# Three score regions side by side in five PSUM banks, and a group's products with v in one batch

## The chip, the cores and the metric

The kernel runs on one core of a Trainium2 chip. The metric is the device time of one execution in microseconds (us); lower is better. The kernel before took 2687.36 us, the median of three runs (2685.77 to 2690.11). The engines named here are TensorE (PE, with its weight loads as PEld), VectorE (DVE), ScalarE (ACT), GpSimd (POOL) and SyncE (SP), which issues loads. [...]

## The reference

A two-layer diffusion block (512 latent tokens, 256 context tokens, width 1024) and then a third layer of recurrent mixers. Only the two attentions matter here. The first layer has 16 query heads of 64 in 4 groups that share keys and values; the second has 16 heads of 96 with keys and values of their own. Both attend without a mask.

```python
def block_attention(q, k, v):            # q (B, Sq, KVH, G, dk); k (B, T, KVH, dk); v (B, T, KVH, dv)
    scale = dk ** -0.5
    qb = jnp.moveaxis(q.reshape(b, nb, Q_BLOCK, kvh, g, dk), 1, 0)     # blocks of 128 queries
    def one_block(qi):
        s = jnp.einsum('bqhgd,bkhd->bhgqk', qi, k, preferred_element_type=jnp.float32) * scale
        p = jax.nn.softmax(s, axis=-1).astype(v.dtype)
        return jnp.einsum('bhgqk,bkhe->bqhge', p, v)
    o = lax.map(one_block, qb)
    return jnp.moveaxis(o, 0, 1).reshape(b, sq, kvh * g * v.shape[-1])

# layer 0: y_lat = block_attention(q_lat, k_all, v_all) @ w_o, y_ctx = block_attention(q_ctx, k_ctx, v_ctx) @ w_o
# layer 1: y_lat alone; k_all holds 512 latent and 256 context keys
```

## The kernel before

Both attentions are run by one function, `attend`, over a list of units. A unit is one block of 128 queries of one head against its 768 keys; four units are a group (`GqaGroup`: four heads that share keys, in the first attention; `MlaHead`: four query blocks of one head, in the second). The first attention has 64 such units and then 16 context units, each two heads against the 256 context keys, of which two are a group. The second has 64 units.

The order is written by hand (`manual_schedule`), as a software pipeline over n. In step n stand, one behind the other:

- the casts out of PSUM that are left from step n-1 (`highs`, on ScalarE, some on VectorE);
- the exponential of unit n-1 (`exps`, ScalarE, L631), which also sums its row;
- the transposes of unit n-4's probabilities (`turn`, TensorE L660, or L653 for context), copied out by ScalarE (four blocks) and VectorE (two) in L661 and L655;
- the scores of unit n (TensorE, L716 or L1013), their row maximum (VectorE, L603) and the scaled negative maximum (L680 or L997);
- the reciprocal of unit n-1's row sum (VectorE, L637) and the scaling of its probabilities (POOL, L640);
- the subtractions left from step n-1 (`late`, VectorE);
- the stage work of step n: the queries of a later group are transposed (L698, cast in L702 and L703, subtracted in L706 and L707); in the second attention K and V (`kproj`, `vproj`), Q (`qproj`) and its turned rope part (`qrot`) of later heads are computed, with copies out of PSUM on ScalarE (L1271, L1284, L1296, L1309) and, for K and Q of the next head, three casts (L1319) and three subtractions (L1323) on VectorE;
- a part of a finished group's products with v (`products`, TensorE L722 or L1021, on half-width tiles of 64 columns), `per` keys in a step: two of six in the first attention, one of two for context, three of six in the second. When the last is done, the cast of the result (ScalarE, L734 or L1034) and the subtraction for its low part (VectorE, L738 or L1040) follow in the next step.

PSUM is laid out by pools: two score tiles `s` of two banks each, used in turn, and four tiles of one bank under the tag `pt`, for transposes, projections and the group's products `ob`. The framework puts in the waits: an instruction waits for those that touch the same tile before it. A wait is left out where an earlier one on the same engine covers it.

Each fp32 product with v is two instructions in the trace, so that a group of six blocks of keys and two halves has 24. Matrix products elsewhere are three instructions each (L139 to L141), of high and low parts.

Of the kernel before, what the change touches and what calls it, by code (L numbers as in the profile page):

```python
# [9 lines left out]
F32 = mybir.dt.float32  # L10
# [6 lines left out]
PSUM = bass.MemoryType.PSUM  # L17
P = 128
# [8 lines left out]
class Bump:  # L27


    def __init__(self, *regions):  # L30
        self.free = list(regions)
        self.tags = {}
# [273 lines left out]
class GqaNet(Base):  # L306
# [103 lines left out]
    def gqa(self):  # L410
        nc, i, tc, flow = self.nc, self.i, self.tc, self.flow
        W = i["gqa_w_qkv"][0]
        with ExitStack() as ph:
# [6 lines left out]
            with tc.tile_pool(name="q0", bufs=1, reuse_waits="tile") as pool, tc.tile_pool(name="q0ps", bufs=2, reuse_waits="tile", space=PSUM) as ps:  # L420
# [46 lines left out]
                b = self.turn_cols(rows, ps, pool, "b")  # L467
# [52 lines left out]
                            flow.add(ada.pop(0))  # L520
                flow.finish()
                self.ada_bufs = 2
            with tc.tile_pool(name="a0", bufs=1, reuse_waits="tile") as pool, tc.tile_pool(name="a0s", bufs=2, reuse_waits="tile", space=PSUM) as pss, \
                    tc.tile_pool(name="a0p", bufs=4, reuse_waits="tile", space=PSUM) as psp:
                units = []
                for ts in (range(4), (4, 5)):
                    for o in range(2):
                        for t in ts:
                            for g in (2 * o, 2 * o + 1):
                                gr = GqaGroup(self, pool, Q, K, V, t, g)  # L530
                                units += [(gr, (x,)) for x in range(4)] if t < 4 else [(gr, (0, 1)), (gr, (2, 3))]
                stages = {}
                none = lambda: None
                for n, (gr, xs) in enumerate(units):
                    if xs[0] == 0:
                        stages.setdefault(n - 3, []).append(gr.prepare(psp))
                n = 8
                for t in range(6):
                    for f in self.q_rope(None, Q, t, 1):
                        stages.setdefault(n, []).append((f, none, none))  # L540
                        n += 2
                ada = self.ada_steps(0, 11, pool, psp, None, True)
                next(ada)
                for x in range(2):
                    stages.setdefault(1 + x, []).insert(0, (lambda: next(ada, None), none, none))
                self.ahead = []
                for x in range(2):
                    for y, f in enumerate(self.out_weights(i["gqa_w_o"][0], x)):
                        stages.setdefault(n - 2 + 6 * x + 2 * y, []).append((f, none, none))
                self.attend(units, pool, pss, psp, stages)  # L550
# [18 lines left out]
    def attend(self, units, pool, pss, psp, stages):  # L569

        nc = self.nc
        N = len(units)
        work, highs, lows = [], [], []
        for n in sorted(k for k in stages if k < 0):
            for fs in stages[n]:
                for f in fs:
                    f()
        with self.tc.manual_schedule():  # L580
            for n in range(N + LAG + 6):
                for f in highs:
                    f()
                highs, late, lows = [], lows, []
                if 1 <= n <= N:
                    self.exps(pool, *units[n - 1])
                if LAG < n <= N + LAG and units[n - LAG - 1][0].last == units[n - LAG - 1][1][-1]:
                    g, xs = units[n - LAG - 1]
                    g.ob = psp.tile([P, 2, 128], F32, name="ob", tag="pt")
                    work.append((g, g.products()))  # L590
                if LAG <= n < N + LAG:
                    g, xs = units[n - LAG]
                    self.turn(pool, psp, g, xs)
                if n < N:
                    g, xs = units[n]
                    s = pss.tile([P, 1024], F32, name="s", tag="s")
                    m = self.sp.tile([P, 3, 2], F32, name="sm", tag="sm", bufs=6)
                    for k, x in enumerate(xs):
                        g.scores(x, s[:, k * g.nk:(k + 1) * g.nk])
                    if n == 0:  # L600

                        nc.scalar.activation(self.sp.tile([P, 1], F32, name="se", tag="se", bufs=1), s[:, :1], AF.Exp, scale=0.0)
                    nc.vector.tensor_reduce(out=m[:, 0, :len(xs)], in_=s[:, :g.nk * len(xs)]  # L603
                                            .rearrange("p (k n) -> p k n", k=len(xs)), axis=AX.X, op=ALU.max)
                    g.sm[xs] = s, m
                    g.bias(xs, m)
                if 1 <= n <= N:
                    self.softmax_end(*units[n - 1])
                for f in late:
                    f()  # L610
                for pe, high, low in stages.get(n, []):
                    pe()
                    highs.append(high)
                    lows.append(low)
                if work:
                    g, fs = work[0]
                    for f in fs[:g.per]:
                        f()
                    del fs[:g.per]
                    if not fs:  # L620
                        work.pop(0)
                        highs.append(g.high)
                        lows.append(g.low)
            assert not work and not highs and not lows

    def exps(self, pool, g, xs):
# [37 lines left out]
class GqaGroup:  # L664


    def __init__(self, net, pool, Q, K, V, t, g):
        self.net, self.pool, self.Q, self.K, self.V, self.t, self.g = net, pool, Q[t], K, V, t, g
        self.c0, self.nk = (0, NL + NC) if t < 4 else (NL, NC)
        self.keys = list(range(6)) if t < 4 else [4, 5]  # L670
        self.p, self.sm, self.last = {}, {}, 3
        self.per = 2 if t < 4 else 1

    def scale(self, x):
        return self.net.RS[:, self.t, 4 * self.g + x:4 * self.g + x + 1]
# [32 lines left out]

        return turn, high, low

    def scores(self, x, s):
        q = self.q[x % 2][:, 128 * (x // 2):128 * (x // 2) + 128]
        for j in range(2):
            for n0 in range(0, self.nk, 512):
                n1 = min(self.nk, n0 + 512)
                self.net.nc.tensor.matmul(s[:, n0:n1], lhsT=q, rhs=self.K[j][:, self.g, self.c0 + n0:self.c0 + n1],  # L716
                                          start=j == 0, stop=j == 1)

# [265 lines left out]
class MlaHead:  # L984

    last = 3
    per = 3

    def __init__(self, m, h):
        self.m, self.net, self.h, self.nk = m, m.net, h, NL + NC  # L990
# [13 lines left out]
            self.pT.append(pool.tile([P, 6, 2, 128], F32, name="pT", tag="pT", bufs=3))  # L1004
        return self.pT[x // 2][:, :, x % 2, :]

    def scores(self, x, s):
        e = self.h % 2
        (qh, ql), (kh, kl) = self.m.Q[e], self.m.K[e]
        c = slice(128 * x, 128 * x + 128)  # L1010
        for k, (a, b) in enumerate(((qh, kh), (qh, kl), (ql, kh))):
            for n0, n1 in ((0, 512), (512, 768)):
                self.net.nc.tensor.matmul(s[:, n0:n1], lhsT=a[:, c], rhs=b[:, n0:n1], start=k == 0, stop=k == 2)  # L1013

    def products(self):
# [32 lines left out]
class MlaNet(MlpNet):  # L1048
    def mla(self):
        nc, i, tc = self.nc, self.i, self.tc  # L1050
        m = Mla(self)
        self.m = m
        with ExitStack() as ph:
            mp = ph.enter_context(tc.tile_pool(name="mp", bufs=1, reuse_waits="tile"))
            tcf = [T.rearrange("p a b -> p (a b)") for T in self.TC]
            xf = self.XN.rearrange("p a b -> p (a b)")
            m.cqT = [mp.tile([P, 3, NL], F32R, name=f"cqT{j}") for j in range(2)]
            m.ckT = [t[:, :1536].rearrange("p (k n) -> p k n", k=2) for t in tcf]
            m.qpe = xf[:, :2048].rearrange("p (t h f) -> p t h f", t=4, h=16)


            kk = mp.tile([P, 2, 2, NL + NC], F32R, name="K")
            m.K = [[kk[:, e, j, :] for j in range(2)] for e in range(2)]
            m.Q = [[tcf[j][:, 1536:] for j in range(2)], [mp.tile([P, NL], F32R, name=f"Q1{j}") for j in range(2)]]
            with tc.tile_pool(name="mA", bufs=1, reuse_waits="tile") as pool:
                self.mla_in(pool, m, kk.rearrange("p e j n -> p (e j n)"))
            self.l0.close()
            with tc.tile_pool(name="a1", bufs=1, reuse_waits="tile") as pool, tc.tile_pool(name="a1s", bufs=2, reuse_waits="tile", space=PSUM) as pss, \
                    tc.tile_pool(name="a1p", bufs=4, reuse_waits="tile", space=PSUM) as psp:
                self.mla_attend(pool, pss, psp, m.cqT, m.ckT, m.qpe, m)  # L1070

    def row_rs(self, pool, x, n):
# [1625 lines left out]
```

## Time and profile before

| | us |
|---|---|
| median of three runs | 2687.36 |
| profiled execution | 2689.55 |
| its span, first to last instruction | 2687.7 |
| TensorE busy in it | 2588.1 (96%) |
| VectorE busy | 1734.3 (65%) |
| ScalarE busy | 1156.9 (43%) |
| POOL busy | 649.7 (24%) |

The profiled execution is 2.2 us above the median, and its time lies 1.9 us above its span. The first attention lies at about 159 to 349 us of the span, the second at about 1064 to 1304. A busy TensorE in the profile is not one at its peak: ends of matmuls are modelled, and matmuls overlap. Of several waits of one instruction the profile names the one that came last.

### The profile page before, as it was taken

How to read it: one execution, taken by the hardware profiler on the slowest of the kernel's cores; microseconds unless marked ns; L12 is line 12 of the kernel's file. 1: busy time of each engine (PE TensorE's matmuls, PEld its weight loads, DVE VectorE, ACT ScalarE, POOL GpSimd, SP SyncE). 2: the span in 40 equal slices, each digit the busy share in tenths (PEclk: the TensorE clock that was granted, in tenths of full speed). 3: DMA queues.
4: the chain of work that ended last, by engine and by line, in shares of the span. 5: the costliest groups of instructions: out<-in, count | busy, mean ns of one | idle time of the engine just before them, and what ended most of it. 6: DMA issues, size and time to landing. Idle time of an engine off the chain costs nothing. (4 is left out here: it accounts for less than half of the span.)

```text
span 2687.7 us, 37906 instructions
## 1 busy us (share of the span) xinstructions
PE 2588.1 (96%) x14954; PEld 2118.7 (79%) x14954; DVE 1734.3 (65%) x3102; ACT 1156.9 (43%) x2016; POOL 649.7 (24%) x541
## 2 busy tenths in 40 slices
PE   8999999999999999999999899989999999999998
PEld 5666689888888898777787678877678888888887
DVE  4458847876666577788488987576675533534445
ACT  4357835333333235655364344253563223532222
POOL 0224322233322013333134445043140011000000
PEclk9999999999999999999999999999999999999999
DMA  8510221333333112000255454234123234222221
GB/s 317 205 32 1 66 92 34 124 120 126 118 122 101 62 39 69 19 33 17 64 166 172 138 174 158 95 107 117 46 68 102 86 94 137 75 94 94 94 94 63
DMA packets 178644, 264.83 MB, mean 99 GB/s; under 512 B 18019, under 2 KB 116954, under 8 KB 177954
## 3 DMA queue, kind: packets, MB, share of 16 engines
q1 hardware_dynamic: 173010, 257.89, 29.0%
q10 hardware_dynamic: 5456, 4.51, 0.6%
q8 instruction: 118, 1.93, 0.3%
q14 instruction: 60, 0.49, 0.1%
HBM read 256.81 MB, written 5.58 MB: 98 GB/s over the span
## 5 line engine op out<-in xcount | busy, mean ns | idle before, releaser
L129 DVE TENSOR_TENSOR wl<-raw,wh 128x1024 fp32r<-128x1024 f32 (+1 forms) x301 | 397.7, 1334 | 358.8 <-ACT wh L126 355.9
L126 ACT CAST wh<-raw 128x1024 fp32r<-128x1024 f32 (+1 forms) x301 | 306.7, 1034 | 618.8 <-PE mm L140 449.7
L139 PE MATMUL mm<-TL,wh 128*128 128x512 f32 (+2 forms) x1512 | 565.7, 375 | 6.1 <-ACT TL L387 4.7
L140 PE MATMUL mm<-TL,wh 128*128 128x512 f32 (+2 forms) x1512 | 561.5, 372 | 4.5 <-DVE TL L388 4.4
L141 PE MATMUL mm<-TL,wl 128*128 128x512 f32 (+2 forms) x1512 | 560.1, 371 | 0.0
L139 PEld LDWEIGHTS mm<-TL,wh 128*128 128x128 f32 (+1 forms) x1512 | 287.2, 190 | 60.5 <-ACT TL L387 5.6
L140 PEld LDWEIGHTS mm<-TL,wh 128*128 128x128 f32 (+1 forms) x1512 | 287.7, 190 | 54.8 <-DVE TL L388 6.0
L141 PEld LDWEIGHTS mm<-TL,wl 128*128 128x128 f32 (+1 forms) x1512 | 287.3, 190 | 52.5
L139 PE MATMUL mm<-TC,wh 128*128 128x256 f32 (+1 forms) x672 | 223.6, 333 | 7.8 <-ACT low L867 7.8
L640 POOL TENSOR_SCALAR p<-p,sm 128x768 f32<-128x768 f32 (+1 forms) x160 | 156.1, 978 | 297.0 <-DVE sm L637 201.9
L141 PE MATMUL mm<-TC,wl 128*128 128x256 f32 (+1 forms) x672 | 223.0, 332 | 0.0
L140 PE MATMUL mm<-TC,wh 128*128 128x256 f32 (+1 forms) x672 | 222.8, 332 | 0.0
L258 POOL TENSOR_TENSOR XN<-XN 128x512 f32<-128x512 f32 x84 | 132.4, 1594 | 282.4 <-ACT XN L251 279.6
L139 PE MATMUL mm<-gh,wh 128*128 128x256 f32 (+1 forms) x544 | 179.7, 330 | 0.3 <-DVE RL L878 0.3
L140 PE MATMUL mm<-gl,wh 128*128 128x256 f32 (+1 forms) x544 | 178.7, 329 | 0.0
L141 PE MATMUL mm<-gh,wl 128*128 128x256 f32 (+1 forms) x544 | 178.1, 328 | 0.0
L258 POOL TENSOR_TENSOR low<-low 128x512 f32<-128x512 f32 x84 | 136.0, 1632 | 152.9 <-ACT low L251 150.1
L603 DVE TENSOR_REDUCE sm<-s 128x1 f32<-128x768 f32 (+1 forms) x144 | 132.7, 922 | 22.5 <-PE s L1013 11.4
L139 PEld LDWEIGHTS mm<-TC,wh 128*128 128x128 f32 x672 | 127.5, 190 | 23.3 <-ACT low L867 9.1
L140 PEld LDWEIGHTS mm<-TC,wh 128*128 128x128 f32 x672 | 127.6, 190 | 13.9
L141 PEld LDWEIGHTS mm<-TC,wl 128*128 128x128 f32 x672 | 127.6, 190 | 12.7
L660 PE MATMUL pt<-ident,p 128*128 128x128 f32 x768 | 116.0, 281 | 17.5 <-ACT pT L661 7.8
(614 smaller groups left out, 4978.8 us busy)
## 6 DMA issues: line engine op xcount, KB each, us to landing
raw<-in_mlp_w_dram SPq DMA_DIRECT2D x64, 1024.0 KB
raw<-in_w_in_dram SPq DMA_DIRECT2D x26, 1024.0 KB
XN<-in_w_ada_dram SPq DMA_DIRECT2D x24, 1024.0 KB
low<-in_ada_w_dram SPq DMA_DIRECT2D x24, 1024.0 KB
raw<-in_ffn_w_in_dram SPq DMA_DIRECT2D x22, 1024.0 KB
adaw<-in_w_ada_dram SPq DMA_DIRECT2D x21, 1024.0 KB
raw<-in_ffn_w_out_dram SPq DMA_DIRECT2D x11, 1024.0 KB
raw<-in_gqa_w_qkv_dram SPq DMA_DIRECT2D x6, 1024.0 KB
```

The costliest lines, as they stand in the source:

```text
L126: nc.scalar.copy(h, v)
L129: nc.vector.tensor_tensor(l, v, h, op=ALU.subtract)
L139: nc.tensor.matmul(out, lhsT=ah, rhs=bh, start=start, stop=False)
L140: nc.tensor.matmul(out, lhsT=ah, rhs=bl, start=False, stop=False)
L141: nc.tensor.matmul(out, lhsT=al, rhs=bh, start=False, stop=stop)
L258: nc.gpsimd.tensor_tensor(rows[k], rows[k], rows[k + h], op=ALU.add)
L603: nc.vector.tensor_reduce(out=m[:, 0, :len(xs)], in_=s[:, :g.nk * len(xs)] .rearrange("p (k n) -> p k n", k=len(xs)), axis=AX.X, op=ALU.max)
L640: nc.gpsimd.tensor_scalar(out=g.p[xs][:, c], in0=g.p[xs][:, c], scalar1=m[:, 2, k:k + 1], scalar2=1.0, op0=ALU.mult, op1=ALU.mult)
L660: nc.tensor.transpose(tp[:, 128 * (x - lo):128 * (x - lo) + 128], p[:, 128 * x:128 * x + 128], self.ident)
```

## The change

There is one PSUM tile S of 2560 columns (five banks) for the whole of an attention. Unit n's scores go to columns 768 (n mod 3) and on: region 0 has bank 0 and the first half of bank 1, region 1 the second half of bank 1 and bank 2, region 2 bank 3 and the first half of bank 4. The products of a group go to the last 256 columns, the second half of bank 4. [...] The products of a group are issued in one step. Tiles under the tag `pt` are three instead of four.

```diff
-            with ... tc.tile_pool(name="a0s", bufs=2, reuse_waits="tile", space=PSUM) as pss, \
-                    tc.tile_pool(name="a0p", bufs=4, reuse_waits="tile", space=PSUM) as psp:
+            with ... tc.tile_pool(name="a0s", bufs=1, reuse_waits="tile", space=PSUM) as pss, \
+                    tc.tile_pool(name="a0p", bufs=3, reuse_waits="tile", space=PSUM) as psp:
...
         work, highs, lows = [], [], []
+
+        S = pss.tile([P, 2560], F32, name="s", tag="s")
...
-                    g.ob = psp.tile([P, 2, 128], F32, name="ob", tag="pt")
+                    g.ob = S[:, 2304:].rearrange("p (a n) -> p a n", a=2)
                     work.append((g, g.products()))
...
-                    s = pss.tile([P, 1024], F32, name="s", tag="s")
+                    c0 = 768 * (n % 3)
+                    s = S[:, c0:c0 + 768]
                     m = self.sp.tile([P, 3, 2], F32, name="sm", tag="sm", bufs=6)
                     for k, x in enumerate(xs):
-                        g.scores(x, s[:, k * g.nk:(k + 1) * g.nk])
+
+                        a, b = c0 + k * g.nk, c0 + (k + 1) * g.nk
+                        cut = min(b, (a // 512 + 1) * 512)
+                        g.scores(x, s[:, k * g.nk:(k + 1) * g.nk], [(p - a, q - a) for p, q in ((a, cut), (cut, b)) if q > p])
...
                 if work:
-                    g, fs = work[0]
-                    for f in fs[:g.per]:
+
+                    g, fs = work.pop(0)
+                    for f in fs:
                         f()
-                    del fs[:g.per]
-                    if not fs:
-                        work.pop(0)
-                        highs.append(g.high)
-                        lows.append(g.low)
+                    highs.append(g.high)
+                    lows.append(g.low)
...
-    def scores(self, x, s):
+    def scores(self, x, s, cuts):
         q = self.q[x % 2][:, 128 * (x // 2):128 * (x // 2) + 128]
         for j in range(2):
-            for n0 in range(0, self.nk, 512):
-                n1 = min(self.nk, n0 + 512)
+            for n0, n1 in cuts:
                 self.net.nc.tensor.matmul(s[:, n0:n1], lhsT=q, rhs=self.K[j][:, self.g, self.c0 + n0:self.c0 + n1],
                                           start=j == 0, stop=j == 1)
```

The same two pool lines change for the second attention, and its `scores`. Line numbers behind the edit move by one to four: the score lines L716 and L1013 become L718 and L1014, the maximum L603 becomes L609, the exponential L631 becomes L635, the products L722 and L1021 become L724 and L1022, their casts L734 and L1034 become L736 and L1035, their subtractions L738 and L1040 become L740 and L1041.

TensorE in the first attention, in the middle of a group, before (`s` scores, `ob` products, `pt` transposes; in brackets the engines whose signals an instruction waits for):

```order
L722 MATMUL ob<-pT,V 64x256 x4
L660 MATMUL pt<-ident,p 128x128 [waits DVE_49,Pool_49]
L660 MATMUL pt<-ident,p 128x128 x3
L660 MATMUL pt<-ident,p 128x128 [waits Activation_49]
L660 MATMUL pt<-ident,p 128x128
L716 MATMUL s<-K_86,q_2105 128x512
L716 MATMUL s<-K_86,q_2105 128x256
L716 MATMUL s<-K_87,q_2105 128x512
L716 MATMUL s<-K_87,q_2105 128x256
L722 MATMUL ob<-pT,V 64x256 x4
L660 MATMUL pt<-ident,p 128x128 [waits DVE_49,Pool_49]
```

And now, in a unit with products:

```order
L718 MATMUL s<-K_86,q_2076 128x512 [waits Activation_49]
L718 MATMUL s<-K_86,q_2076 128x256
L718 MATMUL s<-K_87,q_2076 128x512
L718 MATMUL s<-K_87,q_2076 128x256
L724 MATMUL s<-pT,V 64x256 [waits DVE_49]
L724 MATMUL s<-pT,V 64x256 x11
L664 MATMUL pt<-ident,p 128x128 [waits PE_49,Pool_49]
L664 MATMUL pt<-ident,p 128x128 x3
L664 MATMUL pt<-ident,p 128x128 [waits PE_49]
L664 MATMUL pt<-ident,p 128x128
L718 MATMUL s<-K_86,q_2077 128x512 [waits Activation_49]
```

A product is one instruction in the program's order and two in the trace. Before, four of them stand in each of three steps, and the scores behind the transposes wait for nothing of their own; now all twelve stand in one step, write into S and wait for VectorE, and the next scores wait for ScalarE.

VectorE in the second attention, where a group's products are done, before (L603 maximum, L1323 subtractions for K and Q of the next head, L1040 subtractions of the products):

```order
L997 TENSOR_SCALAR sm<-sm 128x1 [waits DVE_49]
L637 RECIPROCAL sm<-sm 128x1 [waits Activation_49]
L1323 TENSOR_TENSOR K<-kt,K 64x768
L1323 TENSOR_TENSOR Q_9605<-XN,Q_9604 64x512
L1323 TENSOR_TENSOR Q_9605<-row_72,Q_9604 32x512
L661 COPY pT<-pt 128x2x128 [waits PE_49]
L603 TENSOR_REDUCE sm<-s 128x1 [waits PE_49,Pool_49]
L997 TENSOR_SCALAR sm<-sm 128x1 [waits DVE_49]
L637 RECIPROCAL sm<-sm 128x1 [waits Activation_49]
L1040 TENSOR_TENSOR TL_76<-ob,TL_75 64x256 x2
```

And now (the same lines are L609, L1324 and L1041):

```order
L665 COPY pT<-pt 128x2x128 [waits PE_49]
L609 TENSOR_REDUCE sm<-s 128x1 [waits PE_49,Activation_49]
L998 TENSOR_SCALAR sm<-sm 128x1 [waits DVE_49]
L641 RECIPROCAL sm<-sm 128x1
L1324 TENSOR_TENSOR K<-kt,K 64x768
L1324 TENSOR_TENSOR Q_9502<-XN,Q_9501 64x512
L1324 TENSOR_TENSOR Q_9502<-row_72,Q_9501 32x512
L1041 TENSOR_TENSOR TL_76<-s,TL_75 64x256 x2
L665 COPY pT<-pt 128x2x128 [waits PE_49]
L609 TENSOR_REDUCE sm<-s 128x1 [waits PE_49,Activation_49]
```

The subtractions of the products moved up by one unit, behind those for K and Q of the same step, and the maximum waits for ScalarE as well.

## Rows read from the trace of the kernel before

**Rows 1.** view of stretches: engines' busy us, TensorE clock (PEclk), DMA share, GB/s
```profile
158.00:349.00 191.00, 182.96 (x1288) 126.92 (x1289) 164.38 (x420) 151.67 (x348) 84.16 (x102) 1.00 0.13 44
1064.00:1304.00 240.00, 223.78 (x1530) 173.38 (x1528) 190.70 (x401) 139.68 (x300) 82.88 (x67) 0.99 0.09 28
1496.00:1504.00 8.00, 4.40 (x20) 3.03 (x19) 7.69 (x24) 5.36 (x9) 0.00 (x0) 1.00 0.31 100
1552.00:1560.00 8.00, 4.46 (x19) 3.10 (x18) 7.96 (x12) 3.12 (x5) 0.00 (x0) 0.90 0.13 38
```

**Rows 2.** view of waits, TensorE, 158 to 350 us: total us, times, longest
```profile
PE s L716 <- ACT p L631: 2.5, 4, 0.9
```

**Rows 3.** view of the score lines: count, ns min/median/max, first and last start
```profile
L716 PE MATMUL s<-K,q x320: 274/285/505, 158.9 to 341.4; 128*128 128x512 f32 x128, 128*128 128x256 f32 x32
...
L1013 PE MATMUL s<-K,TC x192: 274/388/776, 1064.8 to 1280.2; 128*128 128x512 f32 x96, 128*128 128x256 f32 x96
...
L1013 PE MATMUL s<-K,Q x192: 277/338/505, 1075.7 to 1292.2; 128*128 128x512 f32 x96, 128*128 128x256 f32 x96
```

**Rows 4.** timeline, first attention: start us, duration us, engine, line [idle before <-releaser]
```profile
162.51 0.95 PE L716 MATMUL s<-K,q 128*128 128x512 f32 x4
...
163.50 0.96 DVE L603 TENSOR_REDUCE sm<-s 128x1 f32<-128x768 f32 x1 [0.89 <-PE s L716]
163.70 0.99 ACT L631 ACTIVATE p<-s,sm,RS 128x768 f32<-128x768 f32 x1
...
164.75 0.99 ACT L631 ACTIVATE p<-s,sm,RS 128x768 f32<-128x768 f32 x1
...
164.84 0.96 PE L716 MATMUL s<-K,q 128*128 128x512 f32 x4 [0.94 <-ACT p L631]
```

**Rows 5.** timeline, first attention, around one batch of products
```profile
228.06 0.63 PEld L722 LDWEIGHTS ob<-pT,V 128*64 128x64 f32 x8 [0.25 <-issue]
228.06 1.08 PE L722 MATMUL ob<-pT,V 128*64 128x256 f32 x8
...
229.07 0.64 PEld L660 LDWEIGHTS pt<-ident,p 128*128 128x128 f32 x6 [0.39 <-issue]
...
229.19 0.37 ACT L734 CAST TL<-ob 128x256 fp32r<-128x256 f32 x1 [0.36 <-PE ob L722]
...
232.58 0.40 DVE L738 TENSOR_TENSOR TL<-ob,TL 128x256 fp32r<-128x256 f32 x1
```

**Rows 6.** timeline, first attention, a context unit
```profile
327.43 0.72 PE L716 MATMUL s<-K,q 128*128 128x256 f32 x4
...
328.26 0.69 DVE L603 TENSOR_REDUCE sm<-s 128x2 f32<-128x512 f32 x1 [0.18 <-PE s L716]
```

**Rows 7.** timeline, second attention, around one group
```profile
1175.07 0.96 DVE L603 TENSOR_REDUCE sm<-s 128x1 f32<-128x768 f32 x1 [0.59 <-PE s L1013]
...
1178.90 0.85 DVE L1040 TENSOR_TENSOR TL<-ob,TL 64x256 fp32r<-64x256 f32 x2
...
1181.35 0.90 ACT L631 ACTIVATE p<-s,sm 128x768 f32<-128x768 f32 x1 [2.85 <-DVE sm L637]
...
1185.20 0.74 ACT L1034 CAST TL<-ob 64x256 fp32r<-64x256 f32 x2 [0.92 <-PE ob L1021]
...
1189.77 1.30 PE L1013 MATMUL s<-K,TC 128*128 128x512 f32 x6
...
1193.92 0.59 ACT L1296 COPY XN<-st 128x512 f32<-128x512 f32 x1 [1.51 <-PE st L141]
...
1194.29 1.29 PE L1013 MATMUL s<-K,Q 128*128 128x512 f32 x6
...
1195.69 0.96 DVE L603 TENSOR_REDUCE sm<-s 128x1 f32<-128x768 f32 x1 [0.69 <-PE s L1013]
...
1196.98 1.51 PE L1021 MATMUL ob<-pT,V 128*64 128x256 f32 x12
...
1197.08 1.17 ACT L1309 COPY row<-st 32x512 f32<-32x512 f32 x2 [0.69 <-PE st L1205]
```

More of the change, by code (lines that the diff above doesn't have):

```diff
@@ L522, in gqa @@
                 self.ada_bufs = 2
-            with tc.tile_pool(name="a0", bufs=1, reuse_waits="tile") as pool, tc.tile_pool(name="a0s", bufs=2, reuse_waits="tile", space=PSUM) as pss, \
-                    tc.tile_pool(name="a0p", bufs=4, reuse_waits="tile", space=PSUM) as psp:
+            with tc.tile_pool(name="a0", bufs=1, reuse_waits="tile") as pool, tc.tile_pool(name="a0s", bufs=1, reuse_waits="tile", space=PSUM) as pss, \
+                    tc.tile_pool(name="a0p", bufs=3, reuse_waits="tile", space=PSUM) as psp:
                 units = []
@@ L671, in __init__ @@
         self.p, self.sm, self.last = {}, {}, 3
-        self.per = 2 if t < 4 else 1
     def scale(self, x):
@@ L986 @@
     last = 3
-    per = 3
     def __init__(self, m, h):
@@ L1005, in turned, with scores @@
         return self.pT[x // 2][:, :, x % 2, :]
-    def scores(self, x, s):
+    def scores(self, x, s, cuts):
         e = self.h % 2
@@ L1011, in scores @@
         for k, (a, b) in enumerate(((qh, kh), (qh, kl), (ql, kh))):
-            for n0, n1 in ((0, 512), (512, 768)):
+            for n0, n1 in cuts:
                 self.net.nc.tensor.matmul(s[:, n0:n1], lhsT=a[:, c], rhs=b[:, n0:n1], start=k == 0, stop=k == 2)
@@ L1067, in mla @@
             self.l0.close()
-            with tc.tile_pool(name="a1", bufs=1, reuse_waits="tile") as pool, tc.tile_pool(name="a1s", bufs=2, reuse_waits="tile", space=PSUM) as pss, \
-                    tc.tile_pool(name="a1p", bufs=4, reuse_waits="tile", space=PSUM) as psp:
+            with tc.tile_pool(name="a1", bufs=1, reuse_waits="tile") as pool, tc.tile_pool(name="a1s", bufs=1, reuse_waits="tile", space=PSUM) as pss, \
+                    tc.tile_pool(name="a1p", bufs=3, reuse_waits="tile", space=PSUM) as psp:
                 self.mla_attend(pool, pss, psp, m.cqT, m.ckT, m.qpe, m)
```

## The prediction

> **What bounds the kernel now.** I read the view of stretches first. In both attentions TensorE is the engine that sets the end: it is busy 182.96 of 191 us in the first and 223.78 of 240 us in the second, at a granted clock of 1.00 and 0.99 [rows 1]; VectorE follows with 164.38 and 190.70. Then the view of waits: in the whole first attention TensorE waited for an exponential before its scores four times, 2.5 us in all [rows 2]. The reader is to see that the loop score, row maximum, exponential is hidden today: with two score tiles, unit n writes while the exponential of unit n-1 still reads. The first and last score starts give the pace [rows 3]: 158.9 to about 341.0 us for 80 units (the last row of a unit is about 0.4 us behind its first), so 182.1 us; in the second 1064.8 to about 1291.2 for 64, so 226.4 us.
>
> **What the change does to the waits.** All three score regions and the products' region are now slices of one tile S. In the order of the built program every score batch has a wait on ScalarE of its own, where before it had one in four, since the other three were covered by waits that stood ahead of them. Counted along ScalarE's instructions, the signal waited for is that of the exponential of unit n-1, the one just before, also for region 0 (banks 0 and 1) when that exponential reads region 2 (banks 3 and 4). The third region is thus never used to run ahead: the reader of any part of S holds up the writer of any other. The same count gives three more links: the products wait for the row maximum of unit n that was written just ahead of them; the cast of the products stands ahead of exponential n on ScalarE; and exponential n+1 waits for VectorE's subtraction that reads the products. So the program becomes one serial loop, which I price link by link, from score start to score start.
>
> **The bare unit.** First attention [rows 4]: scores 162.51 to maximum 163.50, 0.99 us; maximum to exponential (164.75), 1.25; exponential 163.70 to the next scores 164.84, which waited for it, 1.14. Sum 3.38 us, where a unit now takes about 2.4. Second attention [rows 7]: scores 1194.29 to maximum 1195.69, 1.40; 1.25 as above; the exponential lasts 0.90, not 0.99, so 1.05 after it. Sum 3.70. A context unit [rows 6]: 0.83 to its maximum of 0.69, then the 0.29 that lie between the end of a maximum and the exponential [rows 4], and 1.14, since its two exponentials have half the width each: 2.95.
>
> **The products, first attention.** One batch of 24 instead of three of 8. Eight take 1.08 us [rows 5] and twelve 1.51 [rows 7], so about 0.104 each further one: 24 take 1.08 + 16 x 0.104 = 2.74. In that unit: 0.99 + 0.96 maximum + 0.05 + 2.74 + 0.04 + 0.38 cast [rows 5] + 1.14 = 6.30. In the next unit the subtraction of 0.40 [rows 5] comes ahead of the exponential: 3.78. A group of four: 6.30 + 3.78 + 2 x 3.38 = 16.84. Eight units run before the first products: 27.0. Fourteen groups: 235.8. Then 16 context units: with a batch of 8, 0.83 + 0.69 + 0.05 + 1.08 + 0.04 + 0.37 + 1.14 = 4.20, the next 2.95 + 0.40 = 3.35; five such pairs 37.75, one pair without products 5.9, two pairs with the last long groups 2 x (7.55 + 1.66) = 18.4; together 62.1, up to the last start 58.7. Sum 321.5 against 182.1: **+139 us**.
>
> **Second attention**, eight units (two heads) at a time, all from [rows 7]. Unit 0 has a product batch of 1.51 + 12 x 0.104 = 2.77 and two casts of 0.74 together: 1.40 + 0.95 + 0.05 + 2.77 + 0.04 + 0.74 + 0.03 + 1.05 = 7.03. Unit 1: three subtractions for K and Q stand ahead of the two that read the products on VectorE; from a maximum at 1175.07 to the end of such a pair at 1179.75 it is 4.68, so 1.40 + 4.68 + 0.05 + 1.05 = 7.18. Unit 3: products for K (six, 256 wide) and Q (nine, 512 wide) follow the scores, and the copy out of them starts 4.15 after the scores (1189.77 to 1193.92), lasts 0.59 and stands ahead of the exponential: 5.82. Unit 2 has six of 512: 1.41 less, 4.40. Unit 4: the turned rope part ends and products start 2.69 after the scores (1194.29 to 1196.98): 2.69 + 2.77 + 0.81 + 1.05 = 7.32. Unit 5 has the two subtractions alone: 3.70 + 0.85 = 4.55. Unit 6 is bare, 3.70. Unit 7 has its maximum late by three subtractions and a copy, an estimate of 0.5: 4.20. Sum 44.2. Six such octets 265.2. The first has no products: 34.7 (its unit 4 ends on the two row copies, 2.79 + 1.17 + 1.05 = 5.0). The last, up to the last start, has only products: 36.9. Sum 336.8 against 226.4: **+110 us**.
>
> **Edits that I cost at nothing.** Cutting scores at the bank edge: 512 + 256 becomes 256 + 512 in every third unit, the same four or six instructions, and a context unit crosses no edge. Three tiles for turned probabilities instead of four: each waits for a copy out that is over a unit old; the idle of TensorE in the loop (some 2 us in a bare unit) covers it. If that cover were gone it would be at most the 0.4 to 0.6 us of a copy per unit, 60 us. POOL's scaling and SP's weight loads keep their place and gain slack. The batch also removes changes between full-width and half-width products: 32 in the first attention's long groups, 8 in its context groups, 16 in the second, 56 in all, each with 0.25 us ahead of the products and 0.39 behind them in which TensorE waited for nothing that the profile shows [rows 5]: 56 x 0.64 = 36 us. That is a gain only where TensorE sets the pace, and in the serial loop it doesn't.
> [...]
>
> **The sum.** 139 + 110 = 249 us on the profiled execution's 2689.55 gives 2939; that execution is 2.2 us above the median of the runs shown, so 2937 there.
>
> **Rivals.**
> Waits by bank: if what counts at run time is only a shared bank, one unit in three (the one that shares bank 1 with its forerunner) is serial and the others overlap as now. A third of 249 is 83, less the 36 of the batch: about 2735. Against it is the count above: region 0 waits for a read of region 2.
> [...]
> Only the bare loop counts: the products, casts and subtractions are hidden after all (their engines have slack). 64 x 3.38 + 15 x 2.95 - 182.1 = 78, and 63 x 3.70 - 226.4 = 7: 2689.6 + 85 = 2775. For it: such work is hidden today. Against it: it stands in the same queue ahead of the exponential.
> Faster: the waits are met early and the removed changes are the whole effect, 2687.4 - 36 = 2651. It is decided at one point: whether an exponential of unit n-1 can end before TensorE reaches scores n. It could only if the work between the two on TensorE were longer than 2.4 us in each unit; transposes are under 1 us.
> Clock: TensorE would be busy for little over half of the time. A stretch so busy (4.40 of 8 us) was granted 1.00, another (4.46 of 8) 0.90 [rows 1]. [...]
>
> **How the numbers follow.** Chances: the sum as worked out 0.80; clock low for half of it or more 0.09; waits by bank 0.04; bare loop 0.04; faster 0.02; no difference 0.01. What a measurement of this kernel tells from no change is about 0.2%, 5 us. So faster 0.02, same 0.01, slower 0.97. The unit of the bare loop may be off by 0.1 us in 144 units (14 us), a unit with products by 0.6 in 40 (24 us), and a clock of 0.9 adds some 25: the range is 2885 to 3010. It leaves out the rivals, 0.2.
>
> **What would show it.** In the profile after: TensorE busy for 50 to 65% of both attentions; nearly every score batch with idle time ended by the exponential's line, in all some 200 us; starts of scores 3.4 us apart in plain units and 6.3 in those with products; first attention from first to last scores 320 us, second 337; no gap before or after products that matters. I am wrong if score batches follow each other without a wait for the exponential, if the row of the products' cast does not delay the exponential behind it, or if the granted clock of the attentions falls to 0.8 or less.

## The result and the profile after

The changed kernel takes **3041.7 us** (median; 3040.05 to 3042.6 in four runs) against 2686.57 of the kernel before in the same measurement: a ratio of 1.132, 95% interval 1.130 to 1.133, or 355 us more. The forecast was 2937 us, 250 us more, with a range up to 3010. The sign and the serial loop are as foretold; some 100 us are missing from the sum.

In its profiled execution (3040.05 us) the two attentions have grown from 182.1 and 226.4 us, first to last score start [rows 3], to 389.3 and 365.2: 346 of the 350.5 us that lie between the two profiled executions. The rest of the kernel is as before. The view of stretches of the changed kernel, both attentions (length; busy us of PE, PEld, DVE, ACT, POOL; granted clock; DMA), against [rows 1]:

```profile
159.00:556.00 397.00, 266.41 (x1258) 181.22 (x1259) 169.08 (x415) 154.85 (x346) 85.58 (x102) 0.69 0.06 19
1265.00:1660.00 395.00, 272.70 (x1601) 207.96 (x1600) 201.97 (x422) 144.37 (x307) 83.12 (x69) 0.89 0.06 18
```

VectorE, ScalarE and POOL are busy for about as long as they were, in stretches that are 206 and 155 us longer. TensorE is busy for 67% and 69%, above my 50 to 65% since its work itself is stretched: the granted clock (the third number from the end), 1.00 and 0.99 before, is 0.69 and 0.89. The first of these is below the 0.8 that the prediction named as a sign of being wrong. The view of waits of the changed kernel, TensorE, the first attention (total us, times, longest) and then the second, against [rows 2]:

```profile
PE s L718 <- ACT p L635: 105.8, 79, 2.6
PE s L724 <- DVE sm L609: 21.8, 21, 1.1
...
PE s L1014 <- ACT p L635: 111.2, 61, 5.5
```

Where TensorE waited four times for an exponential ahead of the first attention's 80 score batches, it does so 79 times now, and 61 times ahead of the second's 64: 217 us. The second line is the link from a row maximum to the products. One group of the first attention, in the timeline of the changed kernel (start, length, engine, line, idle before and what ended it), against [rows 4, 5]:

```profile
253.44 1.65 PE L718 MATMUL s<-K,q 128*128 128x512 f32 x4 [1.23 <-ACT p L635]
255.19 0.96 DVE L609 TENSOR_REDUCE sm<-s 128x1 f32<-128x768 f32 x1 [2.52 <-PE s L718]
...
256.21 4.87 PE L724 MATMUL s<-pT,V 128*64 128x256 f32 x24 [1.12 <-DVE sm L609]
...
261.13 0.37 ACT L736 CAST TL<-s 128x256 fp32r<-128x256 f32 x1 [7.26 <-PE s L724]
261.39 1.00 ACT L635 ACTIVATE p<-s,sm,RS 128x768 f32<-128x768 f32 x1
...
262.54 0.98 PE L718 MATMUL s<-K,q 128*128 128x512 f32 x4 [0.65 <-ACT p L635]
...
264.76 0.40 DVE L740 TENSOR_TENSOR TL<-s,TL 128x256 fp32r<-128x256 f32 x1
...
265.26 0.99 ACT L635 ACTIVATE p<-s,sm,RS 128x768 f32<-128x768 f32 x1 [0.74 <-DVE TL L740]
...
266.39 0.97 PE L718 MATMUL s<-K,q 128*128 128x256 f32 x4 [2.01 <-ACT p L635]
...
267.20 1.44 PE L664 MATMUL pt<-ident,p 128*128 128x128 f32 x6
...
269.87 1.65 PE L718 MATMUL s<-K,q 128*128 128x512 f32 x4 [1.23 <-ACT p L635]
...
274.03 1.65 PE L718 MATMUL s<-K,q 128*128 128x512 f32 x4 [1.23 <-ACT p L635]
```

Every link of the forecast is here: scores behind the exponential, products behind the maximum, cast ahead of the exponential, exponential behind the subtraction. The clock can be read from the same rows: equal work has two lengths. The scores at 262.54 and 266.39 take 0.97 us (0.95 in [rows 4]), and the granted clock from 262 to 267 us is 1.00; those at 269.87, 274.03 and 253.44 take 1.65, and from 270 to 274 us it is 0.50. It falls at about 267, behind a wait of 2.01 us (0.51 from 267.2 to 268.7), and stays low through the waits of the bare units and most of the next 24 products (0.57 over the batch shown, which takes 4.87 us, where I had 2.74); it is back at 1.00 for the transposes behind them (261.0 to 261.9). Ten of the fourteen groups, of 20.5 to 20.7 us, do this.

In the second attention every octet (eight units) behind the first has a fall in the long wait or just behind it, and five of these seven have another at unit 6 (timeline of the changed kernel; the first row is unit 6 of the octet before):

```profile
1397.04 2.29 PE L1014 MATMUL s<-K,Q 128*128 128x256 f32 x6 [2.72 <-ACT p L635]
...
1414.52 1.32 PE L1014 MATMUL s<-K,TC 128*128 128x256 f32 x6 [1.06 <-ACT p L635]
...
1419.99 0.85 DVE L1041 TENSOR_TENSOR TL<-s,TL 64x256 fp32r<-64x256 f32 x2
...
1420.94 0.90 ACT L635 ACTIVATE p<-s,sm 128x768 f32<-128x768 f32 x1 [3.98 <-DVE TL L1041]
...
1421.99 2.29 PE L1014 MATMUL s<-K,TC 128*128 128x512 f32 x6 [4.78 <-ACT p L635]
```

The other rows are my unit 1 (7.47 us from start to start; I had 7.18), and behind it scores of 2.29 us instead of 1.32, at a granted clock of 0.50 (1421.9 to 1424.3) instead of 1.00 (1414.5 to 1416.0).

### The profile page after: what moved, and what is told of

It is laid out like the page before. It is cut to its first block, busy times and chain, and to the rows that moved or that the text cites. A ratio compares the mean times of both kernels' runs of the same rounds, so it can differ in the third digit from the quotient of the medians.

```text
span 3038.2 us, 37985 instructions
## 1 busy us (share of the span) xinstructions
PE 2712.1 (89%) x14954; PEld 2198.3 (72%) x14954; DVE 1743.0 (57%) x3102; ACT 1162.7 (38%) x2016; POOL 647.7 (21%) x541
## 5 line engine op out<-in xcount | busy, mean ns | idle before, releaser
L609 DVE TENSOR_REDUCE sm<-s 128x1 f32<-128x768 f32 (+1 forms) x144 | 133.5, 927 | 249.3 <-PE s L718 137.2
L718 PE MATMUL s<-K,q 128*128 128x256 f32 (+1 forms) x320 | 98.8, 445 | 107.4 <-ACT p L635 105.8
L718 PEld LDWEIGHTS s<-K,q 128*128 128x128 f32 x320 | 63.4, 251 | 136.8 <-ACT p L635 130.9
```

## The experiments

Theory: two causes, the serial loop that the single tile makes, and a clock that falls because the loop leaves TensorE idle. Rivals: the batch does it; the wait goes by banks; the links are longer than I priced. Granted clocks below are those of the first and the second attention.

**1. The batch alone**, in the kernel before.

```diff
-                    g, fs = work[0]
-                    for f in fs[:g.per]:
+                    g, fs = work.pop(0)
+                    for f in fs:
```

> The kernel before with one part of the change alone: a group's products with v are issued in one batch; the score tiles stay two and apart, the products' tile stays by itself. Theory (the serial loop made the change slow, the batch did not): no unit waits for the exponential just ahead of it, so nothing of the 355 us appears. 56 changes between full-width and half-width products go, 0.64 us each, 36 us at most, all of it only if TensorE alone sets the pace; VectorE is busy 86% and 79% of the attentions, so I expect a half of it, 2670 us, between 2650 and 2690. Rival (a long batch holds up the scores of the next unit and so the loop): 24 products of 2.74 us in one unit instead of 1.08 in three; if 1.66 us of that came out in each of 30 groups the time would be 50 us more, 2735.

Measured: 2696.76 us, ratio 1.0034 (1.0020 to 1.0048), 9 us slower, clocks 1.00 and 0.96. That is above the 2690 that I allowed and well below the rival's 2735. No serial loop, as the theory says (scores wait 3.9 and 4.8 us for an exponential), but no gain either. Products and transposes of the first attention, by line (count, busy us, mean ns, idle before), in the kernel before and then in this one:

```profile
L722 PE MATMUL ob<-pT,V 128*64 128x256 f32 x432 | 59.9, 393 | 0.4
L660 PE MATMUL pt<-ident,p 128*128 128x128 f32 x384 | 57.3, 281 | 3.9 <-ACT pT L661 1.5 <-DVE pT L661 1.5 <-DVE TL L738 0.6
```

```profile
L719 PE MATMUL ob<-pT,V 128*64 128x256 f32 x432 | 51.5, 384 | 0.0
L657 PE MATMUL pt<-ident,p 128*128 128x128 f32 x384 | 56.9, 278 | 7.2 <-DVE q L704 3.3 <-DVE pT L658 1.7 <-DVE TL L735 1.6
```

The same 432 products take 8.4 us less for 40 batches fewer, each a change to half width and back: 0.21 us at most, and not 0.64. My 0.25 and 0.39 us were idle time of the weight loads, with matmuls still running: in [rows 5] the products end at 229.14 and the transposes start at 229.07. Even 0.21 is an upper bound, since such rows overlap: from first to last score start TensorE as a whole is busy for 171.6 us, not 174.9, 3.4 us less. Its idle time there grows from 7.2 to 11.8 us, by 3.3 us ahead of the transposes alone, so that this attention is 1.3 us longer and not shorter. The second attention has 7.0 of the 9 us: its clock is lower (0.96 against 0.99), and scores wait 4.8 us for an exponential instead of 1.7.

**2. The regions alone**, products in a tile of their own and in steps.

```diff
-                    g.ob = S[:, 2304:].rearrange("p (a n) -> p a n", a=2)
+                    g.ob = psp.tile([P, 2, 128], F32, name="ob", tag="pt")
...
-                    g, fs = work.pop(0)
-                    for f in fs:
+                    g, fs = work[0]
+                    for f in fs[:g.per]:
...
```

> The changed kernel with the single score tile of three regions, but the products in a tile of their own and in steps of eight or twelve as before. [...] Nearly every score batch's idle time is ended by the exponential. Rival (the batch and its place in the score tile are what costs, three regions in one tile are harmless): within 10 us of before, 2680 to 2697.

Measured: 2870.27 us, ratio 1.068 (1.066 to 1.070), clocks 0.93 and 0.97, within what the theory gave: 2775 us at a full clock, and up to 2900 at the clocks of the changed kernel. The rival falls: the loop without the batch and its links costs 183 us. Where scores wait it is for an exponential, 41 and 52 times (52.8 and 63.0 us); in the first attention the transposes wait too, 17.0 us for ScalarE's copy and 10.3 for the subtraction of the queries, both of which read the three small tiles.

**3. One tile, no shared bank**: the kernel before with its two regions as slices.

```diff
...
+        S = pss.tile([P, 2, 1024], F32, name="s", tag="s")
...
-                    s = pss.tile([P, 1024], F32, name="s", tag="s")
+                    s = S[:, n % 2, :]
...
```

> The kernel before with its two score regions, each still on two banks of its own, declared as two slices of one tile instead of two tiles; the four small PSUM tiles, the cuts, the products and their steps are as before. No bank is shared by two units. Theory (the wait goes by the tile as the program declares it): scores n wait for exponential n-1, and the time is that of the kernel with three regions and stepped products within 30 us, so 2775 to 2900, each score batch's idle time ended by the exponential. Rival (what is waited for goes by the bank or by the region): as before, 2680 to 2695.

Measured: 2859.22 us, ratio 1.064 (1.063 to 1.066), 11 us from run 2; clocks 0.91 and 0.95. Scores wait for an exponential 74 and 51 times (75.3 and 68.8 us). In its timeline, two units on different banks:

```profile
281.28 0.98 PE L717 MATMUL s<-K,q 128*128 128x512 f32 x4 [0.69 <-ACT p L632]
...
282.36 0.96 DVE L604 TENSOR_REDUCE sm<-s 128x1 f32<-128x768 f32 x1 [0.85 <-PE s L717]
...
283.61 0.99 ACT L632 ACTIVATE p<-s,sm,RS 128x768 f32<-128x768 f32 x1 [0.36 <-DVE sm L638]
...
284.74 0.96 PE L717 MATMUL s<-K,q 128*128 128x512 f32 x4 [0.45 <-ACT p L632]
```

The scores at 284.74 write the other two banks and still wait for the exponential of 283.61. The wait goes by the tile as the program declares it (all these pools have `reuse_waits="tile"`; no run shows another setting); 3.46 us from start to start is my bare unit (3.38), with scores of 0.98 and 0.96 us (0.95 in [rows 4]), and the difference is its first link, scores to maximum, 1.08 us and not 0.99.

**4. TensorE kept busy** in the changed kernel.

```diff
+            for _ in range(12 if lo and xs[0] != 1 else 0):
+                nc.tensor.transpose(tp[:, 256:384], self.ident, self.ident)
```

> The changed kernel with twelve more transposes of the identity in every unit that isn't the second of a group, into columns of a turned-probabilities tile that nothing reads: they compute nothing used, and stand on TensorE where it waits for the exponential. Theory (the 104 us by which the forecast was exceeded are the lowered clock, and the clock fell because TensorE was idle in the loop): the granted clock of the attentions returns to 0.95 or more and, although TensorE has more to do, the time falls to 2940 to 2975 us. Rival (the loop's links are longer than I priced at either clock): the clock may rise, but the time stays at 3041 or goes up, by as much as 12 x 0.1 x 110 units = 130 us.

Measured: 2995.21 us, ratio 1.115 (1.113 to 1.117): 46 us faster than the changed kernel with some 1150 transposes more. The expected 2975 was missed: 42 of the 46 us come in the first attention, where the long units are mostly back at a clock of 1.00 and the context units, which have no filling, are not. The second attention, filled in three units of four, goes from 0.89 to 0.93 only and gains 2.5 us. One group in the timeline; then the same stretch of long units in the changed kernel and in this run; then this run's last context units and what follows them:

```profile
262.23 0.98 PE L720 MATMUL s<-K,q 128*128 128x512 f32 x4 [0.54 <-ACT p L635]
...
264.33 2.81 PE L726 MATMUL s<-pT,V 128*64 128x256 f32 x24 [1.12 <-DVE sm L609]
...
268.60 0.97 PE L720 MATMUL s<-K,q 128*128 128x256 f32 x4 [0.65 <-ACT p L635]
...
272.45 0.98 PE L720 MATMUL s<-K,q 128*128 128x512 f32 x4 [0.70 <-ACT p L635]
...
275.94 0.98 PE L720 MATMUL s<-K,q 128*128 128x512 f32 x4 [0.54 <-ACT p L635]
...
279.43 0.97 PE L720 MATMUL s<-K,q 128*128 128x256 f32 x4 [0.54 <-ACT p L635]
```

```profile
239.00:279.00 40.00, 27.41 (x130) 18.82 (x128) 18.18 (x44) 15.02 (x31) 8.35 (x9) 0.67 0.00 1
239.00:279.00 40.00, 32.22 (x245) 26.13 (x243) 22.92 (x56) 17.27 (x35) 10.66 (x11) 1.00 0.00 1
...
479.00:519.00 40.00, 26.52 (x113) 16.61 (x111) 13.57 (x37) 14.26 (x43) 7.45 (x16) 0.57 0.22 80
```

At a clock of 1.00 the starts lie 6.37, 3.85, 3.49 and 3.49 us apart; the forecast had 6.30, 3.78, 3.38 and 3.38. The group is 17.20 us against 16.84 forecast and 20.59 in the changed kernel.

**5. Batch kept, products untied**: the first hunk of run 2 alone.

> The changed kernel with the batch kept, but the products in a small tile of their own, no longer a slice of the score tile. Theory (two of my links tie the products to the loop: the batch waits for the row maximum, the exponential behind waits for the subtraction): the batch starts right behind the scores and the next unit returns to 3.5 us. [...] Rival (the batch itself, wherever it lies, lowers the clock and so makes the rest of the 355 us): above 2990.

Measured: 2936.11 us, ratio 1.093 (1.092 to 1.095). The first attention:

```profile
159.00:507.00 348.00, 243.38 (x1274) 165.03 (x1274) 171.11 (x418) 154.60 (x346) 85.46 (x102) 0.78 0.07 22
```

Both links of the products together cost at least some 105 us in the changed kernel; at least, since here the products take one of the three small tiles, and the transposes wait 15.6 us for the subtraction that reads it. The time is at the upper end of the 2880 to 2940 us that I expected, at a clock of 0.78 and not above 0.85, and between this run and run 2, which differ in the batch alone, lie 66 us (77 between the two profiled executions, 2938.6 and 2861.55). Of the 77, 50 are in the first attention (341.6 against 291.1 from first to last score start) and 23 in the second (321.1 against 298.2). A group where the clock holds is 5.2 + 3 x 3.46 = 15.6 here and 14.5 in run 2, so 15 us for 14 groups; the first attention's clock is 0.93 in run 2 and 0.78 here, and the rest of the 50 goes with it. My reading is that the batch takes work out of the three other units of a group, so that TensorE idles longer there. The timelines fit it (in a mean group TensorE idles 5.3 us here and 4.1 in run 2), but no run shows by itself that this lowers the clock. The rival falls for the bulk and is right in this part.

**6. Five banks as two tiles.**

```diff
-        S = pss.tile([P, 2560], F32, name="s", tag="s")
+        S, S2 = pss.tile([P, 1536], F32, name="s", tag="s"), pss.tile([P, 1024], F32, name="s2", tag="s2")
...
```

> The changed kernel with its five banks declared as two tiles instead of one, regions 0 and 1 in the first, region 2 and the products in the second; the batch is kept. Now only the scores of region 1 wait for the exponential of the unit just before. Theory (the wait goes by the tile): about a third of the units is serial, the others overlap; a third of the 249 us of the loop is 83, and the batch alone cost 9, so 2780 us, between 2735 and 2830, at a granted clock of 0.95 or more in the attentions. Rival (the loop is set by something else in the layout, such as the three small PSUM tiles or the cuts): no better than 2950.

Measured: 2845.93 us, ratio 1.059 (1.058 to 1.061): 196 us less by the declaration alone, with the same columns, batch, cuts and three small tiles. The view of waits, TensorE, first and second attention:

```profile
PE s L718 <- ACT p L635: 37.7, 28, 2.8
...
PE s L718 <- DVE TL L740: 4.2, 5, 0.8
...
PE s L1014 <- ACT p L635: 32.9, 22, 3.4
PE s L1014 <- DVE TL L1041: 12.9, 6, 4.4
```

The waits for an exponential are where the theory has them: of 28 and 22 (79 and 61 in the changed kernel), 27 and 21 stand ahead of the scores of region 1, the only one whose forerunner lies in the same tile. The time is 16 us above the range that I had for it. Its clocks are 0.88 and 0.93, below the 0.95 that I expected, and its scores wait 4.2 and 12.9 us for the subtraction of the products that share the second tile, which I had left out.

**7. Three tiles of two banks**, with the batch, on the kernel before.

```diff
-            ... name="a0s", bufs=2, ...    name="a0p", bufs=4, ...
+            ... name="a0s", bufs=3, ...    name="a0p", bufs=2, ...
...
-                    g.ob = psp.tile([P, 2, 128], F32, name="ob", tag="pt")
+                    g.ob = s[:, 768:].rearrange("p (a n) -> p a n", a=2)
...
```

> The kernel before with a group's products in one batch, three score tiles of two whole banks each, the products in the unused quarter of the score tile of the unit before, and two small PSUM tiles instead of four. Here scores n wait for the exponential n-3 alone. Theory (the batch was no gain alone because TensorE's burst of 2.8 us leaves ScalarE and VectorE without scores, and a third tile lets them be written ahead): no idle time of the score batches is ended by the exponential, and a part of the 36 us of mode changes comes out: 2655 to 2685 us. Rival (with two small PSUM tiles each pair of transposes waits for the copy out of the pair before, 0.4 to 0.6 us in 144 units): 2690 to 2770.

Measured: 2818.62 us, ratio 1.049 (1.048 to 1.051), above both ranges. The view of waits, TensorE, first attention (L657 transposes, L704 subtraction of the queries, L719 products, L628 exponential):

```profile
PE pt L657 <- ACT pT L658: 35.3, 34, 1.8
PE pt L657 <- DVE q L704: 26.5, 17, 1.8
PE s L719 <- ACT p L628: 17.7, 17, 2.0
```

No scores wait for an exponential (0.3 us in the first attention, none in the second), so this run-ahead is there; transposes and products wait instead. With two small tiles the transposes need the copy of the unit just before, which stands on ScalarE behind the exponential, or the subtraction of queries that were turned in such a tile. The products lie in the score tile of the unit before and wait for the exponential that reads it. So there is again a loop, at clocks of 0.89 and 0.96. I had priced the copy alone, not its queue, and left the other two waits out. None of these layouts beats the kernel before.

**8. More filling**, where run 4 left the clock low: the context units (first hunk), and by the query block of a head in the second attention.

```diff
+            for _ in range(0 if xs[0] else 14):
+                nc.tensor.transpose(tp[:, 256:384], self.ident, self.ident)
...
+    def fill(self, x):
+        return (12, 0, 40, 0)[x] if self.h % 2 else (0, 0, 12, 12)[x]
```

> The changed kernel with idle time of TensorE filled as before by transposes of the identity that nothing reads, now also in the context units (14 in every second one) and, in the second attention, 40 in the unit that waits for VectorE's five subtractions, while the two units in which K and Q are made have none. Theory (what was left of the excess is the clock in those places): the granted clock of the context units rises from 0.57 to 0.79 to above 0.9 and they shrink from 79 to about 62 us; the score batch behind the long wait takes 1.3 instead of 2.29 us and an octet 45.5 instead of 47.4; in all 2995 - 17 - 13 = 2965 us. Rival (these units are longer for another reason): 2985 or more.

Measured: 2976.17 us, ratio 1.108 (1.106 to 1.110), 65 us below the changed kernel and below the rival's 2985. The two attentions, and the place of the long wait:

```profile
158.00:509.00 351.00, 271.80 (x1976) 214.07 (x1977) 173.22 (x422) 155.40 (x347) 85.50 (x102) 0.97 0.08 28
...
1218.00:1584.00 366.00, 299.82 (x2122) 245.15 (x2122) 191.90 (x398) 140.47 (x299) 80.76 (x66) 0.97 0.06 19
```

```profile
1356.45 1.31 PE L1024 MATMUL s<-K,TC 128*128 128x256 f32 x6 [1.06 <-ACT p L635]
...
1358.75 4.53 PE L666 MATMUL pt<-ident 128*128 128x128 f32 x40
...
1363.92 1.32 PE L1024 MATMUL s<-K,TC 128*128 128x512 f32 x6 [0.42 <-ACT p L635]
```

The unit with the long wait is as long as before (7.47 us from start to start), but the scores behind it take 1.32 us and the unit 4.28 us (forecast 4.40; 5.6 to 6.5 in seven of eight octets of the changed kernel). The context units shrink to 61.5 us and an octet to 44.9 (expected 62 and 45.5). Of the 11 us above the expected 2965, some 4 are in the first octet, where the clock was still low (0.79) and the filling added to TensorE's work (40.7 us against 37.1 in the changed kernel); the others I can't place.

## Why the prediction was wrong, and where it was right

Times between score starts, worked out from the timelines, in us:

| | forecast | changed kernel | run 8 (clock 0.97) |
|---|---|---|---|
| first eight units | 27.0 | 33.4 | 31.7 |
| 14 groups | 235.8 | 281.7 | 244.3 |
| context, to the last start | 58.7 | 74.3 | 61.5 |
| second attention, first octet | 34.7 | 37.1 | 40.7 |
| six octets | 265.2 | 285.2 | 269.4 |
| last octet | 36.9 | 42.9 | 40.4 |
| sum | 658.3 | 754.6 | 688.0 |

**The failed step** is the one on the clock, which the sum put at full speed: "a clock of 0.9 adds some 25", and the rival "Clock" at a chance of 0.09. The sum was made with durations read where the granted clock was 1.00 and 0.99 [rows 1], while the same text expected TensorE to be busy for 50 to 65% in units that each end in a wait. From [rows 1] I took two stretches of 8 us, one with a clock of 1.00 and one of 0.90, as a sign that it would nearly hold; neither was a loop that waits in every unit for nearly 400 us. It fell to 0.69 and 0.89. No run shows the 25 us for a clock of 0.9, an estimate of mine; what the runs show is stretches at 1.00 and at 0.50, and what equal work takes there: 0.97 and 1.65 us for the scores of a unit in the first attention, 1.32 and 2.29 in the second, and for 24 products 2.81 (run 4) and 4.87 (at 0.57). If the clock had these two levels alone, 62% of the first attention and 22% of the second ran at 0.50 ((1 - clock) / 0.5), an estimate from the mean clocks. Run 8 gives back 65 us of the excess with nothing changed but the filling, which raises the clock from 0.69 and 0.89 to 0.97 and 0.97, and it carries the filling itself, so 65 is the lower end.
In the groups of the first attention the clock fell behind waits of 2.01 us, and the forecast itself had some 2 us of idle time in a bare unit; that should have been weighed.

**The rest of the excess**, at most 30 us (688.0 against 658.3), are links, start-ups and the filling's own cost, which these runs don't part; some 5 us more lie outside the attentions. The links are known from run 4: a bare unit 3.49, not 3.38, a group 17.20, not 16.84, 5 us over 14 groups. Two terms make this up: scores to maximum, 1.08 us in run 3 and not 0.99, and a further product, which I put at 0.104 us where [rows 5, 7] give (1.51 - 1.08) / 4 = 0.1075, so that 24 take 2.80 and not 2.74 (2.81 in run 4). Unit 1 of an octet is 0.3 longer than forecast. In the first octet of run 8 the filling itself costs.

**Right:** serial by the tile and not by the bank (runs 3 and 6), so the rival "waits by bank" falls; "bare loop only" falls too, since run 5, which takes the products out of the loop, is 105 us below the changed kernel. The four links were in the trace at the places named; score waits of 217 us (forecast some 200); cuts and the loss of the fourth small tile, put at nothing, cost about the 11 us between run 2, which has both, and run 3, which has neither. **Right, at a wrong price:** no gain from fewer changes of width. The 36 us of the rival "faster" would have been 56 x 0.21 = 12 at most, and in run 1, where there is no serial loop, none of it shows in the end.

## What to carry to other kernels

Before PSUM regions are laid side by side, find out what the waits go by: in this program a tile that is sliced into regions is one buffer, and it gives no run-ahead, whatever banks the slices lie in (run 3: scores wait for an exponential 74 and 51 times). When a forecast makes TensorE wait in every unit, price a part of its work at the lower clock (0.50 here) in the sum, not as a rival: of the 105 us by which the loss of 355 exceeds the forecast of 250, at least 65 are the clock. A burst that cost 9 us where the engine was busy cost 66 in a loop with idle time, at a lower clock (0.78 against 0.93 in the first attention, runs 5 and 2).

## What the runs showed of the hardware that was not expected

Adding work to TensorE made the kernel faster: 1152 transposes more, 46 us less (run 4). Behind the wait of 4.78 us in an octet the next six matmuls took 2.29 us at a granted clock of 0.50; with 40 transposes in that wait they took 1.32 (run 8). In the changed kernel the clock changed level twice in each group of 20.5 us over some 200 us. A change to half-width products and back costs at most 0.21 us of TensorE here, a third of the idle time that the weight loads show beside it.
